# Tile normalisation split around PSUM evictions, and PE work reordered, in the first projection of a hybrid decoder layer

## Chip, cores, metric

One Trainium2 chip; the program runs on all 8 of its cores, each with tokens of its own and no exchange with the others. The metric is the device time of one execution on the slowest core, in microseconds (us). Executions come fast and slow (in the slow some cores show a lower granted clock); times are compared between fast executions only.

## The reference, cut

```python
def _layer(x, ...):
    h = _rmsnorm(x, g_attn_norm)
    q, k, v, gate_b, gate_c, u_in = jnp.split(h @ w_in, SPLITS, axis=-1)
    attn = attend_fn(q, k, v, attn_sinks)          # sliding window, 4 kv heads of 64
    # [cut: short convolution of gate_c * u_in, two norms, w_out, gated ffn with convolution]
```

Only the first two lines matter here: x is normalised, then multiplied by the k, v and q columns of `w_in`. A core has 1282 token columns, held as five x tiles (258, then four times 256 columns, 2 MB each in HBM, loaded in four pieces) of 16 blocks of 128 features.

## The kernel before

The weights come in slots of 1 MB (bf16, cast by the transfer from 2 MB): slot 0 holds K, slot 1 V, slots 2 and 3 the first q columns, slots 4 to 7 what follows. The norm is split: hT = x * gain goes into the matmuls, and rstd is multiplied into the products when they leave PSUM. For rstd, ACT squares x, DVE adds, PE sums over the features with a matrix of ones, ACT takes Ln and Exp; V needs rstd as a column, which PE makes by small transposing matmuls.

```python
def norm1(t):                                    # x tile t
    for q in range(4):
        for k in range(4 * q, 4 * q + 4):
            T.ts("dve", hT[:, k, a:b], x[:, k, :], col(V_GA + k), None, ALU.mult)
        if q == 0:
            T.act(S4[t], x[:, 0:4, :], AF.Square)
        else:
            T.act(Sq[t], x[:, 4 * q:4 * q + 4, :], AF.Square)
            T.tt("dve", S4[t], S4[t], Sq[t], ALU.add)
    # [cut: two halving adds]

def kv(t):
    # [cut: for tile 0 in quarters]
    p = [k_task(0, t), k_task(1, t)]             # 32 matmuls
    rstd1(t, nb())                               # sum, Ln, Exp, transposes
    flush(p)                                     # K leaves PSUM (DVE)
    flush([v_task(i) for i ...])                 # V matmuls, V leaves PSUM (ACT)

kv(0); norm1(1); kv(1); norm1(2); xload(3, ...)
qs(0, (0, 1)); qs(1, (0, 1)); kv(2); norm1(3)    # qs: q products of a tile
# [cut: loads]
qs(2, (0, 1)); qs(0..2, (2, 3)); kv(3); norm1(4); qs(3, (0, 1)); kv(4); qs(4, (0, 1)) # [cut]
```

Every engine works in the order of these calls; waits between engines are put in by a tracker.

The softmax here doesn't subtract the row's maximum and nothing guards it: scores larger than these inputs give would overflow.

## Time and profile before

| | before |
|---|---|
| time, median of 5 | 1462.27 us (1461.59 to 1563.75) |
| spans of the cores, profiled run | 1454.0 to 1460.8 us |
| PE busy, share of the chain that ended last | 96%, 88% |
| last q product done, mean of 8 cores (the mark) | 117.4 us |

K(t) and V(t) are the K and V products of tile t.

How to read a timeline row: start, duration, engine, line of the program, operation, target and source, shape, count of merged instructions, and in brackets the idle time before with what ended it. All three numbers of time are in us. One line number stands for all matmuls, as a helper issues them.

The window view of core 0 has, for each stretch, its length, the busy time of PE, weight loads (PEld), DVE, ACT and POOL, then the granted PE clock, the share of the DMA engines and GB/s:

```profile
31.00:50.00 19.00, 13.65 (x85) 9.20 (x84) 9.85 (x24) 6.64 (x11) 1.06 (x2) 0.75 0.86 220
64.00:86.00 22.00, 20.42 (x198) 18.03 (x198) 12.51 (x32) 6.84 (x12) 0.53 (x1) 1.00 0.39 119
86.00:118.00 32.00, 29.24 (x240) 24.23 (x241) 14.36 (x36) 8.82 (x17) 1.59 (x3) 0.95 0.42 76
```

In the first of these PE is busy for only 13.65 of 19 us, and its clock is at 0.75 in the mean: waiting and a slow clock come together.

### The profile page before, as it was taken

The numbers are of one execution on the slowest core, as the hardware profiler recorded it, in microseconds if no ns is written. First come the engines' busy times: TensorE is split into PE (matmuls) and PEld (weight loads), VectorE is DVE, ScalarE is ACT, GpSimd is POOL, SyncE is SP. The second block draws the span as 40 slices with busy tenths as digits, with TensorE's granted clock in tenths as the row PEclk, the third lists the DMA queues.
The fourth block names the chain that finished last, engine by engine and source line by source line (L and its number), as shares of the span: only waits on it lengthen the run. The fifth ranks groups of instructions, "written<-read, shape, count | busy, mean of one in ns | idle before, by whom it ended". The sixth has DMA issues, their size and how long they took to land.

```text
span 1460.8 us, 27220 instructions; the slowest of 8 cores (1454.0 to 1460.8 us)
## 1 busy us (share of the span) xinstructions
PE 1401.9 (96%) x11104; PEld 1037.6 (71%) x11124; DVE 951.6 (65%) x1683; ACT 552.2 (38%) x1213; POOL 458.6 (31%) x529
## 2 busy tenths in 40 slices
PE   4899999999999999999999999999999999999995
PEld 2676555566677777777777777777777777777454
DVE  3655563476533369768768778777878655566756
ACT  2433532344343325344344344344344222222235
POOL 0001221122243313223223223222323645566455
PEclk9999999999999999999999999999999999999997
DMA  8819445423699867555555464564444998584607
GB/s 187 235 28 179 82 98 93 71 48 70 132 203 175 217 107 141 119 116 112 117 118 105 114 125 99 105 142 96 84 77 98 261 241 223 93 215 83 109 1 260
DMA packets 49566, 189.11 MB, mean 129 GB/s; under 512 B 4832, under 2 KB 21728, under 8 KB 40416
## 3 DMA queue, kind: packets, MB, share of 16 engines
q0 software_dynamic: 15840, 98.92, 40.4%
q1 hardware_dynamic: 33600, 88.45, 19.2%
q8 instruction: 87, 1.43, 0.4%
q14 instruction: 39, 0.32, 0.1%
HBM read 249.42 MB, written 40.77 MB: 199 GB/s over the span
## 4 chain that ended last, share of the span: by engine, by line
PE 88%; DVE 5%; ACT 3%; DMA 2%; issue 1%; POOL 0%; SPq 0%; DVEq 0%; ACTq 0%; POOLq 0%
PE psb L214 88%; DVE arena L239 3%; ACT arena L235 2%; DMA arena<-win 1%; DMA arena<-xt 1%; DVE arena L258 1%; DMA arena<-wd 1%; DVE psb L239 0%; PE psb L218 0%; POOL arena L239 0%; DVE arena L251 0%; ACT L235 0%; SPq L209 0%; ACT arena L263 0%; ACT psb L235 0%
## 5 line engine op out<-in xcount | busy, mean ns | idle before, releaser
L214 PE MATMUL psb<-arena 128*128 128x288 f16 (+10 forms) x11032 | 1399.1, 288 | 45.1 <-DMA arena<-win 19.8
L214 PEld LDWEIGHTS psb<-arena 128*128 128x128 f16 (+3 forms) x11052 | 1033.0, 99 | 404.8 <-DMA arena<-win 20.8
L239 DVE TENSOR_TENSOR arena<-psb,arena 128x288 f32<-128x288 f32 (+14 forms) x809 | 349.8, 452 | 348.9 <-PE psb L214 323.5
L239 POOL TENSOR_TENSOR arena<-arena 128x288 f32<-128x288 f32 (+11 forms) x398 | 394.4, 1013 | 384.3 <-ACT arena L235 235.9
L239 DVE TENSOR_TENSOR arena<-arena 128x1024 f16<-128x1024 f16 (+15 forms) x538 | 415.1, 784 | 70.1 <-ACT arena L235 57.0
L263 ACT COPY arena<-psb 128x289 f32<-128x289 f32 (+2 forms) x502 | 196.7, 396 | 497.1 <-PE psb L214 441.1
L235 ACT ACTIVATE arena<-arena 128x1184 f32<-128x1184 f32 (+16 forms) x359 | 270.1, 784 | 276.7 <-DVE arena L239 238.8
L258 DVE SCALAR_TENSOR_TENSOR arena<-arena 128x1184 f32<-128x1184 f32 (+2 forms) x136 | 157.5, 1159 | 49.4 <-ACT arena L235 47.0
L235 ACT ACTIVATE arena<-psb,arena 128x256 bf16<-128x256 f32 (+5 forms) x168 | 65.2, 476 | 86.7 <-PE psb L214 86.6
L209 POOL DMA_DIRECT2D arena<-wu x22 | 11.7, 534 | 248.8 <-DVE arena L258 225.8
L209 POOL DMA_DIRECT2D arena<-wg x22 | 12.9, 588 | 156.1 <-PE psb L214 156.1
L251 DVE TENSOR_SCALAR arena<-arena 128x256 bf16<-128x256 f32 (+7 forms) x115 | 37.1, 374 | 20.2 <-DMA arena<-xt 17.9
L209 POOL DMA_DIRECT2D arena<-win x21 | 11.8, 565 | 106.5 <-PE psb L214 61.2
L209 POOL DMA_DIRECT2D arena<-wd x32 | 18.1, 568 | 37.9 <-PE psb L214 35.3
L263 ACT COPY arena<-arena 128x32 f32<-128x32 f32 (+1 forms) x140 | 24.7, 208 | 0.0
L263 ACT CAST arena<-psb 128x512 f16<-128x512 bf16 (+3 forms) x21 | 10.8, 525 | 32.1 <-PE psb L218 31.9
L265 POOL COPY arena<-arena 128x2 f32<-128x2 f32 (+1 forms) x16 | 3.2, 199 | 37.6 <-DVE arena L239 37.6
L258 DVE SCALAR_TENSOR_TENSOR arena<-psb,arena 128x432 f32<-128x432 f32 (+4 forms) x30 | 14.2, 516 | 0.6 <-PE psb L214 0.5
L218 PEld LDWEIGHTS psb<-arena 128*128 128x128 bf16 (+1 forms) x72 | 5.0, 97 | 3.9 <-POOL arena L239 0.8
L273 DVE RECIPROCAL arena<-arena 128x4 f32<-128x4 f32 (+1 forms) x36 | 6.4, 177 | 1.2
L209 POOL DMA_DIRECT2D arena<-cb x1 | 0.5, 530 | 20.6 <-DMA arena<-xt 20.6
L218 PE MATMUL psb<-arena 128*128 128x128 bf16 (+1 forms) x72 | 6.5, 213 | 0.2 <-POOL arena L239 0.2
(15 smaller groups left out, 25.1 us busy)
## 6 DMA issues: line engine op xcount, KB each, us to landing
arena<-wg POOLq DMA_DIRECT2D x22, 1024.0 KB, 11.9
arena<-wu POOLq DMA_DIRECT2D x22, 1024.0 KB, 9.0
arena<-win POOLq DMA_DIRECT2D x17, 1024.0 KB, 12.0
acs<-arena SPq DMA_DIRECT2D x16, 1008.0 KB, 4.5
arena<-acs SPq DMA_DIRECT2D x16, 1008.0 KB, 23.5
arena<-wd POOLq DMA_DIRECT2D x16, 768.0 KB, 12.4
arena<-wd POOLq DMA_DIRECT2D x16, 640.0 KB, 8.1
arena<-x2s SPq DMA_DIRECT2D x16, 576.0 KB, 22.0
```

The costliest lines, as they stand in the source:

```text
L209: return self.add(q, lambda: eo.dma_start(out=out, in_=in_), [in_, *after], [out, *wr], dma=q)
L214: return self.add("pe", lambda: nc.tensor.matmul(out, lhsT, rhs, start=start, stop=stop, **kw), [lhsT, rhs], [out])
L218: return self.add("pe", lambda: nc.tensor.transpose(out, in_, ident), [in_, ident], [out])
L235: return self.add("act", lambda: nc.scalar.activation(out=out, in_=in_, func=func, **kw), rd, wr)
L239: return self.add(eng, lambda: eo.tensor_tensor(out=out, in0=in0, in1=in1, op=op), [in0, in1], [out])
L251: return self.add(eng, lambda: eo.tensor_scalar(out=out, in0=in0, scalar1=s1, scalar2=s2, op0=op0, **kw), rd, [out])
L258: return self.add(eng, lambda: eo.scalar_tensor_tensor(out=out, in0=in0, scalar=scalar, in1=in1, op0=op0, op1=op1), rd, [out])
L263: return self.add("act", lambda: nc.scalar.copy(out=out, in_=in_), [in_], [out])
L265: return self.add(eng, lambda: eo.tensor_copy(out=out, in_=in_), [in_], [out])
L273: return self.add("dve", lambda: nc.vector.reciprocal(out=out, in_=in_), [in_], [out])
```

## The change

Its intent: squares and scalings of the next tile go ahead of the evictions of the tile before (norm1a), the remaining adds behind them (norm1b). V and, for tiles 2 to 4, a Q product stand between K and the sum, another Q product between the sum and the transposes. Dummy matmuls on constants fill PE while it waits for slot 1. Pieces 1 to 3 of x tile 2 wait for slot 2.

```diff
-        S4 = [V(O_Z + 57344, [4, b - a]) for a, b in LX]
-        Sq = [V(O_Z + 57344 + 8192, [4, b - a]) for a, b in LX]
+        S4 = [V(O_Z + 57344 + i % 2 * 12352, [4, b - a]) for i, (a, b) in enumerate(LX)]
+        Sq = [[V(o_, [4, b - a]) for a, b in LX] for o_ in (O_Z + 65536, O_Z + 49536)]
-        def norm1(t):
+        def norm1a(t):
[cut: scalings, as before]
+                T.act(S4[t] if q == 0 else Sq[q % 2][t], x[:, 4 * q:4 * q + 4, :], AF.Square)
+                if q == 1:
+                    T.tt("dve", S4[t], S4[t], Sq[1][t], ALU.add)
+
+        def norm1b(t):
+            for q in (2, 3):
+                T.tt("dve", S4[t], S4[t], Sq[q % 2][t], ALU.add)
[cut: halving adds]
-        T.dma("sp", cfC, cf_d[:, V_N:])
         wput(2, WR4B[2], win_d[2], after=[xq(1, 1)])
-        xload(2, after=[xq(1, 3)])
+        for q in range(4):
+            T.dma("sp", st0[2][:, 4 * q:4 * q + 4, :], xt_d[2][:, 4 * q:4 * q + 4, :],
+                  after=[xq(1, 3)] if q == 0 else [WR4B[2][:, 0:2]])
+        T.dma("sp", cfC, cf_d[:, V_N:])
         def kv(t):
[cut: K in quarters for all tiles now]
+            if t == 0:
+                warm(14)
+                ssum()
+                flush(p)
+                warm(8)
+                rcol1(t, bank)
+                warm(18)
+                return [v_task(i) for i in vs]
+            pv = [v_task(i) for i in vs]
+            if t == 1:
+                ssum(); flush(p); rcol1(t, bank); flush(pv)    # (four lines in the program)
+                return
+            pq = [q_task(0, t, 2, LX)]
+            ssum()
+            flush(p)
+            pq.append(q_task(1, t, 2, LX))
+            rcol1(t, bank)
+            flush(pv)
+            return pq
-        kv(0)
-        norm1(1)
-        kv(1)
-        norm1(2)
+        pv0 = kv(0)
+        norm1a(1)
+        flush(pv0)
+        norm1b(1)
+        kv(1)
[cut: the same for tiles 2 to 4; the load of the g_out row comes earlier]
```

More of the change, by code (lines that the diff above doesn't have):

```diff
@@ L511, in norm1 @@
                     T.ts("dve", hT[:, k, a:b], x[:, k, :], col(V_GA + k), None, ALU.mult)
-                if q == 0:
-                    T.act(S4[t], x[:, 0:4, :], AF.Square)
-                else:
-                    T.act(Sq[t], x[:, 4 * q:4 * q + 4, :], AF.Square)
-                    T.tt("dve", S4[t], S4[t], Sq[t], ALU.add)
+                T.act(S4[t] if q == 0 else Sq[q % 2][t], x[:, 4 * q:4 * q + 4, :], AF.Square)
[4 more added lines that the diff above has]
+                T.tt("dve", S4[t], S4[t], Sq[q % 2][t], ALU.add)
             T.tt("dve", S4[t][:, 0:2, :], S4[t][:, 0:2, :], S4[t][:, 2:4, :], ALU.add)
@@ L522, in rstd1 @@
             W = b - a
-            T.mm(psb[bank][:, 0:W], onesf, S4[t][:, 0, :])
             ln = S4[t][:, 1, :]
@@ L528, in rstd1, with rcol1 @@
             T.act(r1q[:, q0 - 126:b - 126], ln[:, q0 - a:], AF.Exp, scale=-1.0)
+        def rcol1(t, bank):
+            a, b = LX[t]
             tl = [i for i, (c0, c1) in enumerate(VT) if a <= c0 < b]
@@ L547, in build_nc @@
         xload(1, after=[xq(0, 3)])
+        wput(2, WR4B[2], win_d[2], after=[xq(1, 1)])
+        for q in range(4):
+            T.dma("sp", st0[2][:, 4 * q:4 * q + 4, :], xt_d[2][:, 4 * q:4 * q + 4, :],
+                  after=[xq(1, 3)] if q == 0 else [WR4B[2][:, 0:2]])
         T.dma("sp", cfC, cf_d[:, V_N:])
-        wput(2, WR4B[2], win_d[2], after=[xq(1, 1)])
-        xload(2, after=[xq(1, 3)])
         wput(3, WR4B[3], win_d[3], after=[xq(2, 1)])
         T.memset("dve", vtm.rearrange("p i (j d) -> p i j d", j=4)[:, :, :, 64:65], 1.0)
-        norm1(0)
+        norm1a(0)
+        norm1b(0)
         dbank = {"i": 0, "n": 8}
@@ L565, in k_mm, with warm, k_task @@
                 T.mm(ps[:, 0:b - a], wk(0, k, pc), hT[:, k, a:b], start=(k == 0), stop=(k == 15))
-        def k_task(pc, t, ps=None):
+        def warm(n):
+            ps = psb[nb()]
+            w = onesf.bitcast(BF16)
+            for _ in range(n):
+                T.mm(ps[:, 0:256], w[:, 0:128], w)
+        def k_task(pc, t, ps):
             a, b = LX[t]
-            if ps is None:
-                ps = psb[nb()]
-                k_mm(ps, pc, t)
             def post():
@@ L608, in kv, with ssum @@
         def kv(t):
-            if t:
-                p = [k_task(0, t), k_task(1, t)]
-            else:
-                pk = [psb[nb()] for _ in range(2)]
-                for q in range(4):
-                    for pc in range(2):
-                        k_mm(pk[pc], pc, 0, 4 * q, 4 * q + 4)
-                p = [k_task(pc, 0, pk[pc]) for pc in range(2)]
-            rstd1(t, nb())
+            pk = [psb[nb()] for _ in range(2)]
+            for q in range(4):
+                for pc in range(2):
+                    k_mm(pk[pc], pc, t, 4 * q, 4 * q + 4)
+            p = [k_task(pc, t, pk[pc]) for pc in range(2)]
+            vs = [i for i, (c0, c1) in enumerate(VT) if LX[t][0] <= c0 < LX[t][1]]
+            a, b = LX[t]
+            bank = nb()
+            def ssum():
+                T.mm(psb[bank][:, 0:b - a], onesf, S4[t][:, 0, :])
+                rstd1(t, bank)
+            if t == 0:
[14 more added lines that the diff above has]
+            pq = [q_task(0, t, 2, LX)]
+            ssum()
             flush(p)
-            flush([v_task(i) for i, (c0, c1) in enumerate(VT) if LX[t][0] <= c0 < LX[t][1]])
+            pq.append(q_task(1, t, 2, LX))
+            rcol1(t, bank)
+            flush(pv)
+            return pq
         def qs(t, qcs):
             flush([q_task(qc, t, 2 + qc // 2, LX) for qc in qcs])
-        kv(0)
-        norm1(1)
+        pv0 = kv(0)
+        norm1a(1)
+        flush(pv0)
+        norm1b(1)
         kv(1)
-        norm1(2)
         xload(3, after=[xq(2, 3)])
         qs(0, (0, 1))
+        norm1a(2)
         qs(1, (0, 1))
-        kv(2)
-        norm1(3)
+        norm1b(2)
+        pq = kv(2)
+        norm1a(3)
+        flush(pq)
+        norm1b(3)
         xload(4, after=[xq(3, 2)])
@@ L635, in build_nc @@
         T.dma("sp", scT.rearrange("p a b -> p (a b)"), sct_d)
-        qs(2, (0, 1))
+        T.dma("sp", goab, goa_d.partition_broadcast(128), after=[xq(4, 3)])
         for t in range(3):
             qs(t, (2, 3))
-        kv(3)
-        norm1(4)
-        qs(3, (0, 1))
-        kv(4)
+        norm1a(4)
+        pq = kv(3)
+        norm1b(4)
+        flush(pq)
+        pq = kv(4)
+        flush(pq)
         T.dma("sp", kw_d, kf.rearrange("p a b -> p (a b)"))
         T.dma("sp", vw_d, vf.rearrange("p a b -> p (a b)"))
-        qs(4, (0, 1))
         wload(4)
@@ L660, in build_nc @@
         T.act(STs, STs, AF.Exp)
-        T.dma("sp", goab, goa_d.partition_broadcast(128))
         abank = {"i": 0}
```

## The prediction

> **What bounds the kernel now.** I read, in this order: the page (busy shares, chain that ended last), the cores view, the waits of PE, the PE timeline of the first 125 us on all eight cores, then the timelines of the other engines there, and last the groups by shape in short windows.
>
> ```profile
> PE 1401.9 (96%) x11104; PEld 1037.6 (71%) x11124; DVE 951.6 (65%) x1683; ACT 552.2 (38%) x1213; POOL 458.6 (31%) x529
> PE 88%; DVE 5%; ACT 3%; DMA 2%; issue 1%; POOL 0%; SPq 0%; DVEq 0%; ACTq 0%; POOLq 0%
> ```
>
> PE is busy for 96% of the span and is 88% of the chain, so a microsecond of PE gap that goes away early should come off the end. The change touches only the projection of k, v and the first q columns, some 118 us of the 1460.8. In the changed stretch the PE timeline of core 0, the slowest, reads:
>
> ```profile
> 12.53 1.90 PE L214 MATMUL psb<-arena 128*128 128x258 bf16 x8 [12.53 <-DMA arena<-win]
> 15.22 1.90 PE L214 MATMUL psb<-arena 128*128 128x258 bf16 x8 [0.78 <-DMA arena<-win]
> 18.57 3.62 PE L214 MATMUL psb<-arena 128*128 128x258 bf16 x16 [1.45 <-DMA arena<-win]
> 22.58 1.06 PE L214 MATMUL psb<-arena 128*128 128x258 f32 x2 [0.39 <-DVE arena L239]
> 24.66 0.72 PE L214 MATMUL psb<-arena 1*2 1x1 f32 x6 [1.02 <-ACT arena L235]
> 30.37 7.93 PE L214 MATMUL psb<-arena 128*2 128x256 bf16 x56 [5.00 <-DMA arena<-win]
> 41.41 1.18 PE L214 MATMUL psb<-arena 128*128 128x256 bf16 x4 [3.10 <-DVE arena L251]
> 43.82 4.51 PE L214 MATMUL psb<-arena 128*128 128x256 bf16 x22 [1.23 <-DVE arena L251]
> 49.35 13.41 PE L214 MATMUL psb<-arena 1*128 1x1 f32 x132 [1.01 <-ACT arena L235]
> 63.26 0.70 PE L214 MATMUL psb<-arena 128*128 128x256 f32 x2 [0.51 <-DVE arena L239]
> 64.98 20.42 PE L214 MATMUL psb<-arena 1*128 1x1 f32 x198 [1.01 <-ACT arena L235]
> 86.41 9.25 PE L214 MATMUL psb<-arena 1*128 1x1 f32 x80 [1.01 <-ACT arena L235]
> 97.00 4.87 PE L214 MATMUL psb<-arena 128*128 128x256 bf16 x22 [1.34 <-DVE arena L251]
> ```
>
> The bracket is the gap before the row and what ended it. Up to 30.37 us PE waits for weights; that part is bound by transfers. After it the gaps are 3.10, 1.23, 1.01, 0.51, 1.01, 1.01, 1.34 and, at 102.89, once more 1.01 (the row's length there depends on the window, so I leave it out): 10.2 us. They come from DVE and ACT, not from transfers. The reason for the 3.10 is in the whole timeline of core 0:
>
> ```profile
> 35.78 0.48 ACT L235 ACTIVATE arena<-psb,arena 128x256 bf16<-128x256 f32 x1 [1.39 <-PE psb L214]
> 37.84 1.99 ACT L235 ACTIVATE arena<-arena 128x1024 f32<-128x1024 f32 x2
> 39.87 1.22 DVE L239 TENSOR_TENSOR arena<-arena 128x1024 f32<-128x1024 f32 x1 [5.79 <-ACT arena L235]
> 41.01 1.13 DVE L251 TENSOR_SCALAR arena<-arena 128x256 bf16<-128x256 f32 x4
> ```
>
> The squares of x tile 1 (second row) stand on ACT behind the evictions of the V products of tile 0 (first row), which wait for PE. DVE waits 5.79 us for the square, because its add comes before the scaling of the tile's second half, and PE waits for that scaling. In-order queues turn PE's own progress into a PE wait.
>
> **What the Trainium skill says.** "TensorE: Matmul & The Clock Gate", section "Architectural detail", says ACT and DVE take their work strictly in order while PE can only pull weight loads ahead; the four rows agree. The same page, "Part 1: The HAM clock gate", says an idle PE runs at half clock and needs about 3.4 us of sustained work to get the full one. Here, groups by shape in 64 to 86 us and in 30 to 38 us:
>
> ```profile
> L214 PE MATMUL psb<-arena 128*128 128x256 bf16 x160 | 17.8, 272 | 0.0
> L214 PE MATMUL psb<-arena 128*2 128x256 bf16 x16 | 3.5, 406 | 5.0 <-DMA arena<-win 5.0
> ```
>
> That is 17.8/160 = 0.111 us for one 256-column matmul in a dense stretch, and 3.5/16 = 0.22 us just after the 5.0 us gap: the factor of two is there. "DMA: Bandwidth & Descriptors", section "Queues, rings and completion order", says every DMA engine takes turns between the queues that have work, so two tiles in flight slow each other down. The trace agrees in kind: a 1 MB w_in slot takes 12 us to land here, beside x tiles of 2 MB.
>
> **The change part by part.**
> 1. The squares, scalings and the first add of a tile (norm1a) now come ahead of the V or Q evictions of the tile before, the remaining adds (norm1b) after; two square buffers instead of one. K(t) no longer waits for ACT. Removed: 3.10 + 1.23 + 1.34 = 5.7 us of gaps, and the crawl after them: matmuls paced by DVE or at half clock. By 0.111 us each, the 4 in 1.18 us lose 0.7; the 20 bf16 ones in 4.51 us (less 0.7 for the two f32) lose 1.6; the 20 in 4.87 lose 2.0. Sum 4.3 us.
> 2. V and Q products are put between K and the sum over features, and for tiles 2 to 4 one Q product between the sum and the transposed rstd. Removed: 0.51 and three of the four 1.01 us waits, 3.5 us. Tile 1 keeps its 1.01 us, because nothing stands between there.
> 3. 14 + 8 + 18 dummy matmuls fill PE while it waits for the second weight slot at 30.37 us. Their work is in a gap of 0.39 + 1.02 + 5.00 us, so nothing is gained by themselves; the 48 V matmuls that follow should start at full clock: 16 x (0.22 - 0.11) = 1.7 us. If the clock rises halfway in the first 14 (14 x about 0.17 = 2.4 us), the last dummy ends near 29 us on core 0, before the weights; on cores whose weights landed earlier (core 6 had no wait at all) they cost up to 3 us, but those cores are not the slowest (core 6: 1454.0 us).
> 4. Pieces 1 to 3 of x tile 2 are issued only after w_in slot 2 has landed. That slot then comes earlier and the x tile later.
> 5. The constants and the g_out row move in the SP queue; neither is needed in this stretch. I give them 0.
>
> Check by the other way. Work from 30.37 us to the last q product: 560 matmuls of 256 columns x 0.111 = 62.2; 64 of 130 columns, 2.0 us per 32, = 4.0; four times the sum (0.6) and the transpose (0.5) = 4.4; in all 70.6 us. The last slot's load is released by the last q product and goes out at 118.17 us, so the stretch lasts 87.6 us now: 17.0 too many, against 5.7 + 4.3 + 3.5 + 1.7 + 1.0 (kept) = 16.2 by parts. I take 16.5 including the kept one, so 15.5 to win.
>
> What may come back is part 4. With the new order I put K(2) at 30.37 + 5.3 (V0) + 3.6 (K1) + 3.6 (V1) + 2.2 (sum, wait, transpose) + 2.0 + 3.6 (Q) = 50.6 us. Slot 2 is asked for at 33.44:
>
> ```profile
> 33.44 0.53 POOL L209 DMA_DIRECT2D arena<-win  x1 [16.52 <-DMA arena<-xt]
> 48.26 0.53 POOL L209 DMA_DIRECT2D arena<-win  x1 [14.29 <-DMA arena<-xt]
> 35.55 2.19 SPq L209 DMA_DIRECT2D arena<-xt  x4
> ```
>
> (The rows of POOL and SP; the second POOL issue waits for piece 1 of x tile 2, so that piece landed at 48.26 us; the next SP issue puts the landing of piece 2 at 50.4.) Over 0 to 70 us the casting queue used 39.5% of the DMA time for 4.19 MB and the other 47.4% for 10.16 MB, so a slot costs all engines 6.6 us and a 0.5 MB x piece 1.7. In the new order slot 2 shares with one piece only: 33.4 + some 2 us of latency (my estimate from the 9.0 us that the w_up slots of the same size take later, against 6.6 of engine time) + 6.6 + 1.7 = 43.7 us, before Q needs it at 45. Then pieces 1 to 3 of x tile 2 go out, piece 1 lands near 47.5, and slot 3, which is released by it, shares with the rest: the last piece lands at 51 to 53 us. K(2) needs it 2.7 us after its start, plus about 1.2 us of scaling: PE waits 0 to 2 us, I take 1.0. Everything behind it (slot 3 near 60, x tile 3 near 67, needed at 63 and 72) has slack. So 15.5 - 1.0 = 14.5 us on core 0; 15 with the few tenths of f32 work at half clock (1.06 us for two where other cores take 0.70).
>
> **The rivals.**
> A. The gain is bound by transfers: PE only runs into x tiles 2 and 3 and slot 3 earlier. For it: DMA is 85 to 92% busy until 65 us. Against it: the present kernel waits for no transfer after 30.37 us, and behind 33.44 us there are two slots and two x tiles of work, 26.6 us, ending near 62 to 67 us. If it holds, half is lost: 1454 us.
> B. The dummies delay V(0) on every core, as they run at half clock: 40 x 0.22 = 8.8 us plus the sum, from 22.2 us ends at 33 us. That costs 2 to 3 us: 1450 us. Against it: dense work from 18.57 us should have raised the clock by 23 us; cores 4 and 5 ran the f32 pair at that time in 0.70 us, others in 1.23.
> C. The early tile work makes DVE the bound, as all scaling stands ahead of the evictions. DVE is busy 17.6 of 25 us in 40 to 65 us and 15.0 of 25 after; the same work in 15 us less is still under 80%, and eight PSUM banks let PE go on while evictions lag. It would cost 2 to 4 us.
> D. Everything works and x tile 2 is in time, and the clock stays full in 90 to 110 us, where it was 0.91: up to 19 us, 1443 us.
>
> **Range and chances.** 1462.27 - 15.0 = 1447.3, for which I say 1447. The executions before lie within 0.7 us of one another (the slow one apart), so the width is that of my reasoning: D at the low end, B or half of A at the high end: 1442 to 1453. Faster by over 2% means below 1433, 29 us, more than all waste in this stretch after 30.37 us (17 us) and most of that before it: 0.03. Slower by over 2% needs a new wait of 44 us: 0.01. Within 2%: 0.96.
>
> **What would show it.** In the changed kernel's PE timeline of core 0: no gap over 1 us after V(0) but those after tile 1's sum and perhaps in K(2); no row of bf16 matmuls much over 0.12 us each after 30 us; V(0) starts when slot 1 lands and not later; the first load of the B, C, u weights behind K(4) goes out near 87 us instead of 101.81; the stretch from there to the end is as long as before. I am wrong if PE waits for x tiles or slots 2 and 3 by more than 2 us in sum, if the dummies end after slot 1 has landed on the slowest core, if DVE shows no idle time between 45 and 85 us, or if the gain at 118 us is lost again later, which would point to a wait that I see no sign of.

## More of the kernel before

The mark is used all through: slot 7 is asked for when the last q product of the projection has let go of slot 3, so the time of that POOL issue is the time at which the changed stretch ends. From the mark to the end a core takes another 1338 to 1343 us.

The mark also moves with the landing of slot 1, which lets V(0) start and which no part of the change touches; so I give beside it the time from the first matmul of V(0) to the mark (87.8 us on core 0 here, 89.2 on the mean of the cores).

## The result

| | before | changed | changed / before |
|---|---|---|---|
| fast executions | 1458.7 to 1462.8 us | 1445.2 to 1445.9 us | 0.9891 (0.9878 to 0.9903) |
| mark, mean of 8 cores | 117.4 | 101.4; in a second run 100.5 | |
| mark, latest core | 118.8 | 103.9; 103.4 | |
| V(0) to mark, mean | 89.2 | 72.4; 71.9 | |
| mark to end, mean | 1339.7 | 1340.6 (second run, fast) | |

A ratio here is the mean time of the fast executions of one kernel over that of the other in the same rounds, so it isn't quite the ratio of two medians. Five of the ten executions of the changed kernel were slow (1469 to 1531 us), which is why its median, 1469.32 us (over nine of them), is of no use. The ratio on the 1462.14 us of the kernel before in these rounds gives 1446.2 us. That is 16 us won, and the mark moved by 16.0 us (16.9 in the second run): all of it comes from the stretch that was changed, and none is lost behind it. The outputs are right.

The first profile of the changed kernel fell in the slow state (cores 2 to 5 at a clock of 0.97). Its core 0 was not one of the slow ones (clock 0.993, span 1444.1 us). Its PE timeline:

```profile
19.14 4.75 PE L214 MATMUL psb<-arena 128*128 128x258 bf16 x30 [2.18 <-DMA arena<-win]
24.34 17.36 PE L214 MATMUL psb<-arena 128*128 128x258 f32 x148 [0.45 <-DVE arena L239]
42.72 6.89 PE L214 MATMUL psb<-arena 1*128 1x1 f32 x76 [1.01 <-ACT arena L235]
50.56 1.51 PE L214 MATMUL psb<-arena 128*128 128x256 bf16 x8 [0.95 <-DVE arena L251]
52.79 7.45 PE L214 MATMUL psb<-arena 128*128 128x256 bf16 x52 [0.72 <-DVE arena L251]
```

From 24.34 to 41.70 us there is one row with no gap: the sum of tile 0, the dummies, V of tile 0, and K, V and the sum of tile 1. The 5.00 us wait for slot 1 is filled with dummies, and the 3.10 and 1.23 us waits in K(1) are gone. Left are the 1.01 us of tile 1, as predicted, and 0.95 + 0.72 us in K(2), where x tile 2 comes late. Why the waits in K(1) are gone shows in the whole timeline of the same core:

```profile
35.67 1.06 ACT L235 ACTIVATE arena<-arena 128x1024 f32<-128x1024 f32 x1 [1.75 <-DMA arena<-xt]
35.67 1.14 DVE L251 TENSOR_SCALAR arena<-arena 128x256 bf16<-128x256 f32 x4 [0.68 <-DMA arena<-xt]
36.63 1.17 ACT L235 ACTIVATE arena<-psb,arena 2x256 bf16<-2x256 f32 x3
36.73 3.73 DVE L239 TENSOR_TENSOR arena<-arena 128x1024 f32<-128x1024 f32 x4
```

The last square and the last scaling of tile 1 now start in the same instant, when the x piece lands; the V evictions (third row) and the remaining adds (fourth) follow. In the kernel before, DVE waited 5.79 us at this place for ACT. The POOL rows of slot 4's issue, which the last K product releases, on core 0 of the kernel before

```profile
101.81 0.53 POOL L209 DMA_DIRECT2D arena<-win  x1 [31.88 <-PE psb L214]
```

and of the changed kernel

```profile
89.00 0.53 POOL L209 DMA_DIRECT2D arena<-win  x1 [18.30 <-PE psb L214]
```

show 12.8 us won so far on this core, 1.6 of them because slot 1 landed earlier in this execution (V(0) starts at 28.8 us, not 30.4); I had said 87. The windows of core 4, the slowest of the second run, which was fast:

```profile
31.00:50.00 19.00, 17.89 (x174) 15.59 (x174) 10.14 (x25) 7.25 (x13) 0.53 (x1) 1.00 0.73 185
64.00:86.00 22.00, 22.00 (x215) 19.48 (x213) 19.08 (x48) 11.05 (x16) 0.53 (x1) 1.00 0.53 162
86.00:118.00 32.00, 32.00 (x302) 25.24 (x300) 14.86 (x41) 10.15 (x29) 3.17 (x6) 1.00 0.87 146
```

PE is busy for 17.89 us of the first stretch (13.65 before) and for all of the others, and the granted clock is 1.00 in each. DVE has become nearly full in the second (19.08 of 22), yet PE doesn't wait for it.

### The profile page after: what moved, and what is told of

Same layout as the page of the kernel before. It is cut to its first block, busy times and chain, and to the rows that moved or that the text cites. A ratio compares the mean times of both kernels' runs of the same rounds, so it can differ in the third digit from the quotient of the medians.

```text
span 1471.0 us, 27320 instructions; the slowest of 8 cores (1439.0 to 1471.0 us)
## 1 busy us (share of the span) xinstructions
PE 1423.9 (97%) x11164; PEld 1048.4 (71%) x11164; DVE 954.8 (65%) x1683; ACT 551.7 (38%) x1213; POOL 458.1 (31%) x529
## 4 chain that ended last, share of the span: by engine, by line
PE 86%; DMA 6%; DVE 4%; ACT 2%; issue 1%; POOL 0%; SPq 0%; DVEq 0%; ACTq 0%; POOLq 0%
PE psb L214 86%; DVE arena L239 3%; DMA arena<-win 3%; DMA arena<-xt 2%; ACT arena L235 1%; DVE arena L258 1%; DMA arena<-wd 1%; DVE psb L239 0%; PE psb L218 0%; POOL arena L239 0%; ACT arena L263 0%; SPq L209 0%; ACT L235 0%; DVE arena L251 0%; ACT psb L235 0%
## 5 line engine op out<-in xcount | busy, mean ns | idle before, releaser
L214 PE MATMUL psb<-arena 128*128 128x288 f16 (+9 forms) x11092 | 1421.5, 291 | 32.3 <-DMA arena<-win 17.1
L214 PEld LDWEIGHTS psb<-arena 128*128 128x128 f16 (+2 forms) x11092 | 1043.8, 99 | 403.6 <-DMA arena<-win 18.7
L209 POOL DMA_DIRECT2D arena<-win x21 | 11.8, 563 | 90.4 <-DMA arena<-xt 46.4
## 6 DMA issues: line engine op xcount, KB each, us to landing
arena<-win POOLq DMA_DIRECT2D x17, 1024.0 KB, 11.8
```

Source lines behind the costliest of these rows:

```text
L209: return self.add(q, lambda: eo.dma_start(out=out, in_=in_), [in_, *after], [out, *wr], dma=q)
L214: return self.add("pe", lambda: nc.tensor.matmul(out, lhsT, rhs, start=start, stop=stop, **kw), [lhsT, rhs], [out])
```

## The experiments

Each kernel is the changed one or the one before with one thing undone or done alone. The table has the mark, the time from V(0) to the mark, the sum of PE's gaps of 0.15 us and more from 33 us to the mark (all three means of eight cores), and the ratio to the kernel before with its 95% interval.

| run | mark | latest core | V(0) to mark | gaps | ratio |
|---|---|---|---|---|---|
| kernel before | 117.4 | 118.8 | 89.2 | 10.5 | 1 |
| changed, first / second run | 101.4 / 100.5 | 103.9 / 103.4 | 72.4 / 71.9 | 1.7 / 1.4 | 0.9891 (0.9878 to 0.9903) / 0.9880 (0.9856 to 0.9904) |
| changed, no dummies | 102.2 | 104.1 | 73.2 | 1.1 | 0.9891 (0.9876 to 0.9907) |
| changed, old transfer order | 102.0 | 103.9 | 72.3 | 1.8 | 0.9890 (0.9869 to 0.9911) |
| norm part alone | 115.0 | 116.4 | 85.4 | 7.2 | 0.9978 (0.9960 to 0.9996) |
| PE order alone | 116.5 | 118.2 | 87.3 | 8.5 | 0.9989 (0.9967 to 1.0011) |
| before, dummies in its gaps | 115.5 | 117.7 | 86.8 | 2.1 | slow chip |
| changed, transposes not filled | 104.4 | 106.2 | 75.1 | 4.3 | slow chip |
| changed, slot 2 in quarters | 103.6 | 108.8 | 74.4 | 2.7 | slow chip |
| changed, old norm | 114.2 | 116.5 | 85.4 | 8.4 | slow chip |
| changed, slot 2 earlier | 100.6 | 102.5 | 71.5 | 0.7 | 0.9884 (0.9865 to 0.9904) |
| changed, old norm body at new place (flawed) | 107.3 | 110.0 | 78.4 | 6.0 | 0.9939 (0.9921 to 0.9956) |
| the same, own sums | 103.7 | 106.7 | 74.9 | 3.4 | 0.9919 (0.9898 to 0.9940) |

Two cautions. The mark depends on when transfers land: the changed kernel's two runs differ by 0.9 us, so I read no difference under about 1 us. Slot 1 landed at 27.6 to 29.5 us on the mean of the cores, from run to run; the column from V(0) leaves that out, and also what the dummies cost before V(0). And four kernels ran on a chip on which every execution was slow, of the kernel before too (1547 us and more); their times are not used. Their marks are: the clock drops only later there. The mean granted clock of the eight cores from 34 to 118 us was 1.00 in every window that I took of the run without filling, and 0.97 from 300 to 400 us.

**Without the dummies.**

```diff
-            for _ in range(n):
+            for _ in range(0):
                 T.mm(ps[:, 0:256], w[:, 0:128], w)
```

> The changed kernel without its 40 dummy matmuls (the banks keep their turn). Measure: the time at which w_in slot 7 is asked for, which the last q product releases (mean of the eight cores: 117.4 us before, 101.4 changed), and the fast-run ratio. My theory: the 16 two-row V matmuls after the weight wait run at half clock again (3.5 us instead of 1.9), so the mark comes 1.5 to 2.5 us later on cores that wait over 3 us for slot 1, mean about 102.9; ratio to before about 0.990. Rival (tile x 1 sets the pace behind V(0), so its clock doesn't matter): mark 101.4, within 0.5. Rival (the dummies delay V(0) on most cores): mark 1 us earlier, near 100.4.

The mark came 0.8 us later than in the first run of the changed kernel, 1.6 later than in the second; the ratio is the same, 0.9891. Groups by shape of core 0 in 27 to 36 us, without the dummies

```profile
L214 PE MATMUL psb<-arena 128*2 128x256 bf16 x16 | 3.5, 412 | 2.3 <-DMA arena<-win 2.3
```

and in the changed kernel's second run

```profile
L214 PE MATMUL psb<-arena 128*2 128x256 bf16 x16 | 1.9, 272 | 0.0
```

show the local effect: 3.5 us against 1.9, the 1.6 us that I had worked out. At the end of the stretch 0.8 to 1.6 us of it is seen, no more than the marks scatter, and in the time nothing is resolved.

The dummies also have a cost, which I had overlooked. In the first run of the changed kernel slot 1 had landed before they were through on five of the eight cores, by 0.1 to 2.8 us; in the second run on all eight, by 0.2 to 1.9 us. On core 3 of the first run slot 1 was asked for at 15.27 us and took 10.2 us to land, so it lay there at 25.5 us. The third line is the group of dummies between 25.5 and 28.3 us, where V(0) starts:

```profile
15.27 0.53 POOL L209 DMA_DIRECT2D arena<-win  x1 [11.40 <-DMA arena<-xt]
arena<-win POOLq DMA_DIRECT2D x1, 1024.0 KB, 10.2
L214 PE MATMUL psb<-arena 128*128 128x256 bf16 x18 | 2.1, 273 | 0.0
```

On the mean of the cores V(0) starts 0.9 and 1.0 us after slot 1 has landed, without the dummies 0.1 us; from V(0) to the mark the dummies win 0.8 and 1.3 us. Gain and cost are about equal, which fits the equal ratios.

**Old transfer order.**

```diff
+        T.dma("sp", cfC, cf_d[:, V_N:])
         wput(2, WR4B[2], win_d[2], after=[xq(1, 1)])
-        for q in range(4):
-            T.dma("sp", st0[2]..., after=[xq(1, 3)] if q == 0 else [WR4B[2][:, 0:2]])
-        T.dma("sp", cfC, cf_d[:, V_N:])
+        xload(2, after=[xq(1, 3)])
```

> The changed kernel with x tile 2, slot 2 and the constants issued in the order of the kernel before. My theory: holding x tile 2 back costs what the changed trace shows in K(2) on cores 0, 4, 5 and 7 (gaps of 0.4 to 1.7 us and a stretch at half clock); without it those gaps go, the mark (last q product) falls from a mean of 101.4 to about 100 and on the latest core from 103.9 to about 101. Rival (the order was needed: slot 2 then comes later than the first Q product wants it): a gap of 1 to 3 us that ends with a w_in transfer appears at 43 to 46 us on most cores, and the mark is the same or later, 101.5 to 103.

My theory missed. The gaps in K(2) went, but on six of eight cores PE now waited 0.3 to 2.0 us for slot 2 before the first Q product (over 1 us on three of them), as the rival said in kind. Mark 102.0, ratio 0.9890: the new order moves a wait of some 1 us from one transfer to another and is worth nothing that these runs resolve.

**The norm part alone.**

```diff
 kernel before, with norm1a / norm1b and their places; K, sum, transposes, V, Q in the old order
-        kv(0); norm1(1)
+        pv0 = kv(0); norm1a(1); flush(pv0); norm1b(1)
 [and so for tiles 2 to 4; no dummies, old transfer order]
```

> Only the new order of squares, scalings and adds (norm1a, norm1b, two buffers each); K, sum, transpose, V, Q in the old order, no dummies, old transfer order. My theory: this part is worth 10 of the 16 us: the 3.1, 1.2 and 1.3 us gaps and the slow matmuls behind them go, the gaps of 1.0 us stay (the sum may even wait longer, as its adds come later): mark near 107.5, ratio about 0.993. Rival (the parts are not additive: the sum's wait takes the place of K's wait, since the adds now come last): mark 111 to 114, ratio 0.996 to 0.998.

The timeline of core 0:

```profile
59.25 0.70 PE L214 MATMUL psb<-arena 128*128 128x256 f32 x2 [2.28 <-DVE arena L239]
60.96 22.04 PE L214 MATMUL psb<-arena 1*128 1x1 f32 x198 [1.01 <-ACT arena L235]
84.78 13.24 PE L214 MATMUL psb<-arena 1*128 1x1 f32 x102 [1.78 <-ACT arena L235]
```

The waits for scalings in K are gone, but the sum of tile 2 waits 2.28 us where it waited 0.51 (on three cores that of tile 1 waits, too, 0.3 to 0.5 us): the adds that it needs now come last on DVE, and in the old order PE has nothing else to do between K and the sum. The 1.78 us in the third row were 1.01: Ln and Exp of tile 3 now stand on ACT behind a square of tile 4. The clock, too, stays low behind these gaps: the mean of the cores was 0.87 in 44 to 64 and 0.88 in 84 to 98 us. Mark 115.0: 2.4 us won instead of the 10 that I had given it (3.8 from V(0), as slot 1 landed late in this run; the ratio's 0.22% is 3.2 us). The rival was right in kind, and by the mark the loss was larger still than it said.

**The PE order alone.**

```diff
 changed kernel, with the old norm1 behind the evictions; no dummies, old transfer order
-        norm1a(1); flush(pv0); norm1b(1); kv(1)
+        flush(pv0); norm1(1); kv(1); norm1(2)
```

> Only the new order of PE (V and Q between K and the sum, Q between sum and transpose); the squares and adds as before, no dummies, old transfer order. My theory: takes away 0.5 and three of four 1.0 us gaps, 3.5 us: mark near 114, ratio about 0.9975; the gaps that end with the scaling of x tile 1 and 4 stay at 3.1, 1.2 and 1.3 us. Rival (V behind K also fills what K waited for, so this alone does most of it): mark 106 to 109 and no gap over 1.2 us. Rival (it does nothing alone, PE waits just as long for scalings): mark 117.

The timeline of core 0:

```profile
41.10 1.50 PE L214 MATMUL psb<-arena 128*128 128x256 bf16 x8 [2.23 <-DVE arena L251]
43.51 6.86 PE L214 MATMUL psb<-arena 128*128 128x256 bf16 x42 [0.91 <-DVE arena L251]
79.47 13.97 PE L214 MATMUL psb<-arena 128*128 128x256 bf16 x118 [1.71 <-DVE arena L239]
95.63 1.51 PE L214 MATMUL psb<-arena 128*128 128x256 bf16 x8 [2.19 <-DVE arena L251]
```

K(1) and K(4) still wait for scalings (2.23 + 0.91 us where it was 3.10 + 1.23, and 2.19 + 0.90 where it was 1.34), and a new wait of 1.71 us for evictions behind the adds appears: this run has the whole norm of tile 3 ahead of the evictions of tile 2's Q products. Mark 116.5, 0.9 us won where I had said 3.5 (1.9 from V(0)); the ratio's interval includes 1. Not tested: the old norm behind those Q evictions, and K in quarters, which belongs to this part, by itself.

**The norm part taken out of the changed kernel.** The edit is that of the run before, with dummies and new transfer order kept.

> The changed kernel with the squares, scalings and adds put back as they were before (one buffer each, behind the evictions); PE order, dummies and transfer order stay. With the run that had the PE order alone (mark 116.5) and the one with the norm part alone (115.0) it tells whether the parts add up. If the two parts only work together (theory now): mark 115 to 117, waits of 2.2, 0.9, 1.7, 2.2 us in K of tiles 1 and 4 and in the sum as with the PE order alone. If they added up as predicted (10 us for the norm part): mark 111.4.

Mark 114.2, somewhat below the 115 to 117 of my theory, with gaps of 2.2, 0.9, 1.7 and 2.2 us as with the PE order alone. So the norm part is worth 2.4 us (3.8 from V(0)) where it is put in alone and 13 us (114.2 to 101.4 or 100.5; the same from V(0)) where everything else is there. The parts don't add up: 2.4 + 0.9 us alone, 15.2 us together (117.4 to 102.2, the run without dummies); from V(0) it is 3.8 + 1.9 against 16.0. The single runs have the old transfer order and the joint one the new, which the run above found worth nothing.

**Dummies in the gaps of the kernel before.**

```diff
         def k_mm(ps, pc, t, k0=0, k1=16):
             for k in range(k0, k1):
+                if pc == 0 and (t, k) in DUM:       # {(1, 8): 26, (1, 12): 10, (4, 8): 2, (4, 12): 12}
+                    warm(DUM[t, k])
[in rstd1, between the sum and the transposes:]
+            if t:
+                warm(8)
```

> The kernel before with dummy matmuls put into its PE gaps from tile 1 on (26 and 10 in K of tile 1, 2 and 12 in K of tile 4, 8 between every sum and its transpose): every wait stays, only the array is kept working. It tells what of the 16 us is waiting and what is the half clock that follows a wait. My theory now (a gap of 1 to 3 us also costs as much again at half clock behind it): no slice at half clock after 40 us, mark (last q product) 2 to 4 us earlier than 117.4, ratio 0.997 to 0.9985. Rival (the slow rows are only DVE's pace and the clock has no part in it): mark 117 to 118.5, ratio 1.000.

Counted from V(0), squares and scalings come no sooner (DVE's first add behind the wait for ACT at 9.5 us in both, core 0), yet the mark falls by 1.9 us to 115.5 (2.4 from V(0)). In the window 34 to 44 us the mean granted clock of the cores is 0.99 (0.78 in the kernel before), and 1.00 in 98 to 118 (0.92). So of the 16 us about 2 are the half clock behind the waits, at the low edge of what I had expected and less than the 4.3 us of slow rows that the prediction put in one sum. Much of the rest of those rows is DVE's pace: on core 0 the four matmuls after each wait in K(1) still start 0.26 us apart at full clock, as far apart as the scalings, where dense ones start 0.11 apart.

**Transposes not filled.**

```diff
             flush(p)
-            pq.append(q_task(1, t, 2, LX))
             rcol1(t, bank)
+            pq.append(q_task(1, t, 2, LX))
```

> The changed kernel with the transposes right behind the sum for tiles 2 to 4, the second Q product after them. My prediction gave this filling 1.0 us for each of three tiles. My theory: three gaps of 1.0 us come back and nothing else, mark 104.4. Rival (each gap also trips the clock): mark 106 to 108. Rival (the gap is absorbed later, as PE runs into transfers anyway): mark 101.4 to 102.5.

The timeline of core 2:

```profile
58.62 20.42 PE L214 MATMUL psb<-arena 1*128 1x1 f32 x198 [1.01 <-ACT arena L235]
80.05 11.62 PE L214 MATMUL psb<-arena 1*128 1x1 f32 x102 [1.01 <-ACT arena L235]
92.69 11.49 PE L214 MATMUL psb<-arena 1*128 1x1 f32 x106 [1.01 <-ACT arena L235]
```

Three gaps of 1.01 us are back and the mark is 104.4, 3.0 us later than in the first run of the changed kernel and 3.9 later than in the second (2.7 and 3.2 from V(0)), at a clock of 1.00 throughout. This term of the prediction was right, and a lone gap of 1.0 us in dense work here costs 1.0 us and no clock.

**A candidate: slot 2 in quarters.**

```diff
-        wput(2, WR4B[2], win_d[2], after=[xq(1, 1)])
+        for q in range(4):
+            T.dma("pool", WR4B[2][:, q * 1024:(q + 1) * 1024], ..., after=[xq(1, 1)])
[x piece q of tile 2 waits for quarter q - 1; the first Q product stands before tile 1's transposes]
```

> A candidate: the changed kernel with w_in slot 2 loaded in quarters, each x piece of tile 2 released by a quarter of it and not by the whole, and the first Q product of tile 0 between the sum and the transposes of tile 1. Theory: DMA has no pause around slot 2 any more, Q starts as soon as the first quarter lands, the 1.0 us wait of tile 1 and the waits in K(2) go: mark 99.5 to 100.5, latest core under 102, ratio about 0.988. Rival (transfers set the pace there whatever their order): mark 101.5 as in the changed kernel, with a wait of 1 to 2 us for slot 2 in place of the others.

Worse: mark 103.6, latest core 108.8. On core 0

```profile
47.15 57.12 PE L214 MATMUL psb<-arena 128*128 128x130 bf16 x507 [3.84 <-DMA arena<-win]
```

PE waits 3.84 us for slot 2 (core 7 waits 2.10 and 3.51). From the first issue to the last landing slot 2 takes 12.3 to 16.8 us here, 9.4 to 11.8 in the first run of the changed kernel: the x pieces, released earlier, are in flight with the later quarters. Whether four small transfers are slower by themselves was not tested. In this finer scheme, then, slot 2 had better go first, even if that won nothing against the old order.

**A second candidate: slot 2 asked for earlier.**

```diff
-        wput(2, WR4B[2], win_d[2], after=[xq(1, 1)])
+        wput(2, WR4B[2], win_d[2], after=[xq(1, 0)])
[the first Q product of tile 0 stands before tile 1's transposes, as above]
```

> A second candidate, after the finer slot 2 made Q wait up to 3.8 us: the changed kernel's rule (slot 2 alone, then the x pieces) is kept, but slot 2 is asked for when piece 0 of x tile 1 has landed, not piece 1, so the engines don't run dry in between; the first Q product of tile 0 stands between the sum and the transposes of tile 1. Theory: slot 2 lands about 1.5 us earlier, x tile 2 with it, tile 1's 1.0 us gap and most of the waits in K(2) go: mean mark 99.5 to 100.5 against 101.4. Rival (slot 2 then slows x tile 1 and K(1) waits for it): mark 101 to 102 with a gap before 40 us.

Gaps fall from 1.4 (the second run of the changed kernel, same chip and rounds) to 0.7 us, and three cores have none at all, but the mark is 100.6 against 100.5 and the ratio 0.9884 against 0.9880. On three cores a wait for slot 2 (0.2 to 1.4 us) takes the place of tile 1's gap. But slot 2 was not really asked for earlier: its issue came at 30.9 us on the mean of the cores, against 30.7 in the second run of the changed kernel, since the first piece of x tile 1 landed 1.6 us later in this execution. What an earlier slot 2 is worth stays open. No version here beats the changed kernel beyond the scatter.

**The changed kernel again.**

> The changed kernel once more on this chip, to see how far the mark moves by itself: 101.4 plus or minus 1.0 for the mean of the cores, gaps in K(2) where x tile 2 lands late, no slice at half clock after 34 us on most cores.

Mark 100.5, ratio 0.9880, gaps in K(2) on three of the eight cores. This gives the scatter used above.

**Old norm body at the new place, with a flaw.**

```diff
 changed kernel; norm1a = the old norm1 (one Sq buffer, every add between the scalings), norm1b empty
+        S4 = [V(O_Z + 57344, [4, b - a]) for a, b in LX]           # one buffer: the flaw
```

> The changed kernel with the old body of the norm (one square buffer, each add between the scalings) at the new place, ahead of the evictions. It splits the norm part in two: the place, and the holding back of the last adds. My theory: the place does most of it, since the ACT wait behind the evictions was the cause; K waits about 1.2 us more for one add in tile 1, the sum less: mark 102 to 104. Rival (holding back is what counts): mark over 108.

Mark 107.3, between my theory and the rival. On core 4

```profile
82.00 8.20 PE L214 MATMUL psb<-arena 128*128 128x256 f32 x54 [2.68 <-DVE arena L239]
```

the sum of tile 3 waits 2.68 us for adds of tile 4, because norm1a(4) now comes ahead of that sum and the one buffer is overwritten. Tile 3 was then scaled with tile 4's rstd; the random tokens have nearly the same norm, so the comparison still passed. The result is to be thrown away, but it shows why the change alternates between two S4 buffers.

**The same with sums of its own.**

```diff
-        S4 = [V(O_Z + 57344, [4, b - a]) for a, b in LX]
+        S4 = [V(O_Z + 57344 + i % 2 * 12352, [4, b - a]) for i, (a, b) in enumerate(LX)]
```

> The run with the old norm body at the new place had a flaw of mine: with one buffer for the sums, tile 4's squares overwrite tile 3's sum before PE reads it (tile 3 was scaled by tile 4's rstd, close enough to pass the comparison), and the sum of tile 3 waited 2.7 us for tile 4's adds. Here the sums alternate between two buffers as in the changed kernel; the rest is the same. My theory (the place does most of it): the 2.7 us gap near 82 to 87 us goes, with the half clock behind it, mark 102.5 to 104.5 against 107.3; a gap of 1.7 us before K of tile 3 stays. Rival (holding back the last adds is worth more): mark still over 106.

Mark 103.7, the 2.7 us gap gone, the 1.7 us one still there, as expected. Against the run with the old norm at the old place (114.2) the place alone brings 10.5 us (from V(0), too: 85.4 to 74.9); holding back the last adds and the second square buffer bring the other 2 to 3 (103.7 to 101.4 or 100.5).

## Why the prediction was right, and where not

- **The time** was right: 1447 said, 1446.2 from the ratio, and the chance of a change within 2% too. It was right because the win came from the difference between what the stretch takes (87.8 us on core 0; the prediction's 87.6 is a slip) and the work in it (70.6 us), which needs no split into causes: the four cores of the first run that waited for nothing but tile 1's 1.0 us took 71.0 us from V(0) to the mark. The mean mark moved by 16.0 and 16.9 us in the two runs where I had said 15, and the 1340 us behind it didn't change. There is luck in how close it came: the 1.7 us for the dummies did not come, but the other cores had up to 2.2 us more to lose than core 0, which I had worked from (core 0's own mark moved by 14.3 us in the first run and by 19.4 in the second).
- **Parts 1 and 2, the attribution, failed.** The step was to count for each part the gaps that it would remove, as if the other were there: 10.0 us for the norm, 3.5 for the PE order. Alone they bring 2.4 and 0.9 by the mark (3.8 and 1.9 from V(0)); 10 to 12 of some 16 us need both. The trace of the kernel before shows each gap with the wait that ended last. Behind it stood a second wait: with scalings early, the sum waits for the late adds unless PE has V to do; with V between, K still waits for scalings that are behind the evictions.
- **The slow rows,** 4.3 us in the same term, were put down to DVE's pace or the half clock without a split; about 2 us are the clock.
- **Part 3, the dummies,** failed as a gain: the 1.7 us were there where I looked (1.6 on core 0), but the dummies delay V(0) by 0.9 to 1.0 us on the mean of the cores, and nothing is resolved in the time. I had put that cost on cores that are not the slowest; in the second run it was 0.7 us on core 4, the slowest, so one of my signs of being wrong came.
- **Part 4:** the wait in K(2) was named and its size roughly right (1.67 us on core 0 in the first run, 1.87 on core 4 in the second, none on half of the cores; I had put 0 to 2). On core 4 of the first run the waits for x tile 2 and slots 2 and 3 came to 2.43 us, over the 2 us that were to show me wrong. Not foreseen: behind the wait core 0's clock fell to 0.57 for a slice, and the matmuls went at the pace of late scalings. I had counted such slow rows for the old waits and not for this one: core 0 took 75.1 us from V(0) to the mark, 4.1 more than the cores without a wait. On the mean of the cores that is 1.4 and 0.9 us, near the 1.0 that I had taken. The old order would have cost the same through slot 2. (A slot costs 6.9 us by the prediction's own 39.5% of 70 us for four, not 6.6; nothing hangs on it.)
- **The rivals:** A didn't come. B came in part: the dummies do delay V(0) on most cores, by 0.9 to 1.0 us in the mean and not by 2 to 3. C's premise did, DVE at 19.08 of 22 us where I had said under 80%, without its cost; that the eight PSUM banks carried the lag is likely but not tested. D's clock in 90 to 110 us came.
- **Core 0** was not slowest by nature: in the second run it was core 4.

The window view of core 0 of the changed kernel, first run, around the waits in K(2):

```profile
48.00:52.00 4.00, 3.05 (x23) 1.87 (x21) 1.85 (x5) 1.60 (x2) 0.53 (x1) 1.00 0.88 334
52.00:56.00 4.00, 3.28 (x16) 2.06 (x16) 4.00 (x12) 1.57 (x2) 0.00 (x0) 0.57 0.89 127
```

PE was idle for about 1 us in the first slice, in pieces, and got 0.57 of its clock in the second.

## What to carry to other kernels

Where a stretch is late because in-order queues hold up one another, size the win by the stretch (time taken less work), and expect the single fixes to give little until all links of the loop are cut: here 2.4 and 0.9 us alone, 15.2 together (3.8, 1.9 and 16.0 from V(0)). Put what the next tile needs ahead of the evictions of this one, and what is needed last (the adds) behind; give the array other work to do while they run. Fill a wait with dummies only as far as it surely lasts: here they overran the landing on most cores and won nothing. Check that buffers still alternate where a step was moved ahead of a reader, since a comparison on random data may not notice.

## What the Trainium skill lacked or had wrong

- "TensorE: Matmul & The Clock Gate", section "HAM oscillation", warns of idle gaps over about 3.4 us. Here far shorter ones were followed by a low clock: 0.95 + 0.72 us of gaps with slow rows between, and then a slice at 0.57 (changed kernel, core 0); gaps of 2.28 and 1.01 us in the norm part alone, with a mean of 0.87 in 44 to 64 us. But 1.15 + 0.72 us kept 1.00 (second run, core 4), and so did single gaps of 1.01 us in dense work (transposes not filled) and one of 1.97 us (old transfer order, core 7), where one of 1.55 us was followed by 0.57 in 46 to 50 us (the same run, core 0). The page speaks of micro-idles between matmul groups, too, but has no length for them; in these runs the length alone does not decide.
- The same page, section "Seeing it yourself", says to budget 1.95 GHz for dense matmuls on all cores, with whole dies throttled. In fast executions all eight cores here had a mean granted clock of 0.983 to 0.996; in the profiled executions of the slow chip 0.92 to 0.95. Only in the slowest executions (1686 to 1715 us) was one die at 0.81 to 0.85, near the page's figure. In the slow profile of the changed kernel cores 2 to 5 were at 0.972 to 0.976 and cores 0, 1, 6 and 7 at 0.993 to 0.995, which isn't cores 0 to 3 against 4 to 7.
- "DMA: Bandwidth & Descriptors", section "Queues, rings and completion order", describes turn-taking between queues and no cost of it. Here a slot asked for in quarters beside x pieces took 12.3 to 16.8 us to land, and PE waited 3.84 us for it on core 0; the undivided slot with the x pieces held back took 9.4 to 11.8 us, and PE waited for it only on core 4, 1.06 us.
